# First MLP matrix with three 256-column matmuls per k-tile and a ScalarE rectifier

## The chip, the core and the metric

The kernel runs on one NeuronCore of a Trainium2 chip. The metric is the device time of one execution in microseconds (us), median of several runs; lower is better. Engines are called as in the profile: PE is TensorE (PEld its weight loads), DVE is VectorE, ACT is ScalarE, POOL is GpSimd, SP issues the transfers.

## What is computed

Two layers over 256 tokens of 1024 channels in float32. Each layer has three token mixers (pooling, sparse attention, gated linear attention), a gated merge, an output projection, a squared-ReLU MLP and a gated input embedding. What matters here is the MLP:

```
D_MODEL, SEQ, DEPTH, D_FF = 1024, 256, 2, 4096
h += relu(rmsnorm(h, norm_ffn[i]) @ w_ff1[i]) ** 2 @ w_ff2[i]
```

## The kernel before, in words

Every large product is made of reduced-precision matmuls on split operands: x = high + low, w = high + low, and x·w is taken as high·high + high·low + low·high, all accumulated in PSUM.

Weights come as units of one megabyte (four k-tiles of 128 rows by 512 columns). `prefetch` (L168) loads a unit, `high` (L176) makes the high parts of half a unit on ACT (L180), `low` (L183) the low parts on DVE (L186). At most eight halves are alive (`HL_BUFS`). `step` (L1184) is called after every second k-tile pair of a `Group` and after every `Columns`, and issues at most one low, one high and the loads that are due; so this preparation is interleaved with the rest of each engine's stream, which every engine runs in order.

Two kinds of items run on PE. A `Group` (L1276 to L1278) has the activations as the stationary side and 512 weight columns streaming: three matmuls per k-tile. A `Columns` (L1255 to L1268) is used only for the first MLP matrix. It has 128 weight columns as the stationary side and streams a tile `X[k]` of 512 columns: [high of 256 tokens | low of 256 tokens], made by `norm_x` (L260). Per k-tile it has two matmuls: the weights' high part `wh` against all 512 columns (L1263 or L1266), and the weights' low part `wl` against the first 256 (L1264). So the accumulator `box` takes a whole PSUM bank: columns 0 to 255 hold high·high + low·high, columns 256 to 511 hold high·low.

`hidden(j)` (L1007) makes 512 hidden units: two units of `w_ff1`, four column blocks c, and for each c two `Columns` (kh = 0, 1) of four k-tiles. There are 8 values of j in each of 2 layers, so 16 such blocks of 32 k-tiles. After each c, `post` (L1012) adds the two halves of the bank: ACT copies the second half (L1017), DVE adds the first to it (L1018). After each odd c it works on the pair of column blocks, a tile z of 512: DVE makes max(z, 0)·z (L1020), and `split` makes the high part on ACT (L226) and the low part on DVE (L228). These are `L.f[j, c // 2]`, the stationary side of the second matrix. `ff2_group` (L1026) are Groups for that matrix, into four accumulators `ybox` that stay open for all j. The order of the items is hidden(0), hidden(1), four ff2 groups of j = 0, hidden(2), four ff2 groups of j = 1, and so on, so a block of ff2 groups comes one hidden block after its inputs were begun. Work tiles (`wt`) come from a pool of 47; PSUM has 8 banks.

Of the kernel before, what the change touches and what calls it, by code (L numbers as in the profile page):

```python
# [23 lines left out]

# columns of w_in
C_U, C_Q, C_KV, C_QK, C_V, C_AR, C_GM = 0, 512, 1024, 1816, 2328, 2840, 3368

# columns of the constant tile
K_ID, K_CAUS, K_GLA, K_CMP, K_SEL, K_INV, K_N = 0, 128, 256, 384, 416, 418, 426
# [46 lines left out]
class Unit:  # L76
    """One megabyte of weights, four slots of [128, 512], as high and low parts."""

# [14 lines left out]
class Columns:  # L93
    """128 columns of a unit as the stationary side, the activations of both token tiles streaming"""

# [13 lines left out]
def trunk(tc, x, p, positions, norm_mix, w_in, pool_w, pool_scale, cmp_pos_k, cmp_w_k, cmp_pos_v,  # L109
# [10 lines left out]
    with es:  # L120
# [24 lines left out]

# [1 line left out]
        h = [cp.tile([128, D], F32, name=f"h{t}") for t in range(2)]  # L147
# [13 lines left out]
        def gain(key, k):  # L161
            """a norm's gain, channels [128 k, 128 k + 128)"""
            kind, i = key
            c = 8 * i + k
            return mixg[:, c:c + 1] if kind == "mix" else cols[:, {"ffn": 76, "ple": 92}[kind] + c:][:, 0:1]

# [1 line left out]
        def prefetch(u):  # L168
# [18 lines left out]

# [1 line left out]
        def newton(y, nh, tmp, engine=None, wide=False):  # L189
            """y := (-2 nh)^(-1/2)"""  # L190
            ts(y.bitcast(I32), nh.bitcast(I32), 1, None, op0=ALU.logical_shift_right)
            ts(y.bitcast(I32), y.bitcast(I32), -1, MAGIC, op0=ALU.mult, op1=ALU.add)
            for _ in range(3):
                if engine is not None:
                    engine.tensor_tensor(tmp, y, y, op=ALU.mult)
                    engine.tensor_scalar(tmp, tmp, nh, 1.5, op0=ALU.mult, op1=ALU.add)
                    engine.tensor_tensor(y, y, tmp, op=ALU.mult)
                    continue
                if wide:
                    tt(tmp, y, y, op=ALU.mult)  # L200
                    tt(tmp, tmp, nh, op=ALU.mult)
                else:
                    stt(tmp, y, nh, y, op0=ALU.mult, op1=ALU.mult)
                stt(y, tmp, 1.5, y, op0=ALU.add, op1=ALU.mult)
# [7 lines left out]
        def rstd(s):  # L212
            """s[:, 4:5] := (mean + eps)^(-1/2), the mean being s[:, 1:2] + s[:, 2:3] - eps"""
            ts(s[:, 3:4], s[:, 1:2], s[:, 2:3], -0.5, op0=ALU.add, op1=ALU.mult)
            newton(s[:, 4:5], s[:, 3:4], s[:, 5:6])

        def split_t(src, scale=1.0):
            """transpose of [128 tokens, 512] as four [128, 128], split into high and low"""
            q = ps()
# [12 lines left out]

        # A row's factor 1/rms commutes with the products: rows enter them as h * gain, and what
        # leaves them is scaled on its way out of PSUM.
        aT = {}
# [8 lines left out]
        def gained(q, key, c, out):  # L244
            """high and low parts of q * gain; out(part, k) is where a k-tile's part goes"""
            for part in range(2):
# [13 lines left out]
        def norm_x(t, key, X):  # L260
            """as norm_t, into a tile of [(part, token tile), token] per k-tile, for streaming"""
            for c in range(2):
# [19 lines left out]

# [1 line left out]
        sides = []  # L284
# [36 lines left out]
        def chunk(key, us, post, n=512, ts_=(0, 1), kts=8):  # L321
            """groups of a chunk of n columns over the k-tiles of the units us, one list per token tile"""
            res = []
# [9 lines left out]

# [1 line left out]
        def rope_setup():  # L335
# [41 lines left out]
        def rotate(xv, t):  # L377
            """first 16 of each 64 of [128, 8, 64], in place"""
            tmp = wt().rearrange("p (a n c j) -> p a n c j", a=4, n=8, c=2)
# [5 lines left out]

# [1 line left out]
        def pool_gen(L, i):  # L387
# [32 lines left out]

# [1 line left out]
        def att_gen(L, i):  # L422
# [8 lines left out]
            yield 2  # L431
            # compression blocks: [(parity, d), pair of tokens, key or value, (g, n)], pairs in two tiles
            xs = [wt() for _ in range(2)]
# [3 lines left out]
            for kv in range(2):  # L437
# [14 lines left out]
                yield 1  # L452
            # queries and keys, channels on partitions
            qT = []
# [12 lines left out]
            yield 1  # L467
            # compressed keys (partitions 0-63) and values (64-127), one pass over both weights
            q = ps()
# [27 lines left out]
            def weigh(ev, sm, th):  # L497
                """ev := ev * gate / sum, without the gate's factor 1/2"""
                ts(sm, sm, 1e-30, None, op0=ALU.max)  # L499
# [3 lines left out]

            # compressed branch
            ce = []
            for t in range(2):
# [16 lines left out]
                nc.vector.tensor_reduce(sm, ev, axis=AX.X, op=ALU.add)  # L523
                # the blocks are in (i, g) order, the gates in (g, i) order
                weigh(e.rearrange("p (i g c) -> p i g c", i=4, g=2), sm.rearrange("p (i g) -> p i g", i=4),
# [13 lines left out]

            # selected and window branches  # L540
            work = [(0, g, (2 * a, 2 * a + 1)) for a in range(2) for g in range(2)]
# [74 lines left out]

# [1 line left out]
        def gla_gen(L, i):  # L618
# [62 lines left out]
            for par in range(2):  # L681
# [10 lines left out]
                yield 6  # L692
            # states, one head's rows over its own columns, zeros elsewhere
            state = [wt() for _ in range(3)]
# [64 lines left out]

# [1 line left out]
        def emb_gen(L, i):  # L761
# [9 lines left out]

# [1 line left out]
        def layer(i):  # L773
# [12 lines left out]

            # mixer inputs
            def post_q(t, q):
# [119 lines left out]
            def branch(br, name, attr, first, ns=(0, 1)):  # L908
                for n in ns:
                    if br == 1:  # L910
                        # k-tile i: the heads i and 4 + i
                        wr = w_branch[i, br][:, n * 512:(n + 1) * 512].rearrange("(g i d) n -> g d i n", g=2, i=4)
# [16 lines left out]

            # u, q, ...: inputs of the mixers; G, H, I: gates of the three branches; g, h, i: the branches  # L930
            for c in SEQ:
# [14 lines left out]

            # output projection
            L.mT = {}
# [32 lines left out]

            # product of the input embedding
            X = []
# [19 lines left out]

            # MLP, its hidden units on partitions; 1/rms squared is applied to what it returns
            ybox = {(t, n): Box() for t in range(2) for n in range(2)}

            def hidden(j):  # L1007
                us = two(w_ff1[i], j * 512)
                for c in range(4):
                    box = Box()  # L1010

                    def post(c=c, box=box):  # L1012
                        q = box.ps
                        if c % 2 == 0:
                            L.z = wt()
                        z, zc = L.z, L.z[:, c % 2 * 256:c % 2 * 256 + 256]
                        act(zc, q[:, 256:512], AF.Copy)  # L1017
                        tt(zc, zc, q[:, 0:256], op=ALU.add)  # L1018
                        if c % 2:
                            stt(z, z, 0.0, z, op0=ALU.max, op1=ALU.mult)  # L1020
                            L.f[j, c // 2] = split(z)
                    for kh in range(2):
                        items.append(Columns(us[kh], c, (lambda s, kh=kh: X[4 * kh + s]), (box, 512), kh == 0, kh == 1,
                                             post if kh else None))
# [28 lines left out]

            # gated input embedding
            def post_g(n):
# [8 lines left out]
            def post_last(t, c0, n, box):  # L1064
                """residual, and the final norm of the columns [c0, c0 + n)"""
                s = wt()[:, 0:n]
# [107 lines left out]
        def next_high(n):  # L1174
            """the next half's high part, if it lies near enough and buffers are free"""
            nonlocal n_hi, live
# [17 lines left out]

# [1 line left out]
        mixr = wt()  # L1196
# [49 lines left out]
        for it in items:  # L1246
# [4 lines left out]
            box, n = it.acc  # L1251
            if it.first:
                box.ps_full = ps()
                box.ps = box.ps_full[:, 0:n]
            if isinstance(it, Columns):  # L1255
                cc = slice(it.c * 128, (it.c + 1) * 128)
                for s in range(4):
# [3 lines left out]
                    x = it.rhs(s)  # L1261
                    if s == 0:
                        mm(box.ps, wh, x, start=it.first, stop=False)  # L1263
                    mm(box.ps[:, 0:256], wl, x[:, 0:256], start=False, stop=False)  # L1264
                    if s > 0:
                        mm(box.ps, wh, x, start=False, stop=(it.last and s == 3))  # L1266
                step(at)
# [41 lines left out]
```

## Time and profile before

| | us |
|---|---|
| median of 3 runs | 944.71 |
| lowest and highest | 943.97, 945.86 |
| span of the profiled execution, first to last instruction | 943.0 |
| PE busy, share of the span | 925.8 (98%) |
| DVE busy | 670.5 (71%) |
| ACT busy | 487.7 (52%) |
| both MLP stages, from the first matmul of the first matrix to the last of the second | 174.51 each |

The time of the profiled execution is its span and what lies ahead of the first and behind the last instruction, which the profile does not show. A matmul's row in the trace lasts longer than the time until the next one starts, since they are pipelined: what a matmul costs is read as the distance from its start to the next start. Granted clock 1.00 is 2.4 GHz.

### The profile page before, as it was taken

What the parts mean: (1) busy time and instruction counts of PE and PEld (TensorE: products, weight loads), DVE (VectorE), ACT (ScalarE), POOL (GpSimd) and SP (SyncE); (2) the same over time, 40 slices, a digit from 0 to 9 for tenths busy, and PEclk for the clock granted to TensorE, in tenths of its full rate; (3) what the DMA queues carried; (4) which work ended last, traced back from release to release, by engine and by line L of the source; (5) the groups of instructions that cost most, each with busy time, mean ns of one, the idle gap of its engine ahead of it and who ended that gap; (6) DMA issues with size and microseconds to landing.
All of it is one profiled execution on the core that took longest, in us unless ns stands there. A gap on an engine that the chain in (4) does not pass through costs nothing.

```text
span 943.0 us, 12676 instructions
## 1 busy us (share of the span) xinstructions
PE 925.8 (98%) x4848; PEld 764.5 (81%) x4848; DVE 670.5 (71%) x1203; ACT 487.7 (52%) x833; POOL 16.3 (2%) x37
## 2 busy tenths in 40 slices
PE   6999999999999999999999999999999999999996
PEld 5888877778788888888889887777878888888885
DVE  4976877769667766666886877766885776666675
ACT  5664655454366544444765545544443754555453
POOL 1000000000000000000000000000000000000003
PEclk9999999999999999999999999999999999999998
DMA  7686452336543755555257834534354375555541
GB/s 257 220 257 193 134 167 102 94 94 215 179 163 109 273 201 189 184 199 201 90 151 261 236 95 173 165 119 118 115 198 134 134 243 203 179 179 179 180 154 46
DMA packets 92180, 159.92 MB, mean 170 GB/s; under 512 B 11708, under 2 KB 20056, under 8 KB 92120
## 3 DMA queue, kind: packets, MB, share of 16 engines
q1 hardware_dynamic: 92120, 159.12, 51.1%
q8 instruction: 38, 0.62, 0.3%
q14 instruction: 22, 0.18, 0.1%
HBM read 158.06 MB, written 1.05 MB: 169 GB/s over the span
## 4 chain that ended last, share of the span: by engine, by line
PE 96%; DVE 1%; ACT 1%; DMA 1%; issue 0%; SPq 0%; DVEq 0%
PE ps L1276 22%; PE ps L1278 22%; PE ps L1277 22%; PE ps L1266 10%; PE ps L1264 6%; PE ps L1263 3%; PE ps L600 1%; PE ps L577 1%; PE ps L554 1%; PE ps L241 1%; PE ps L471 1%; PE ps L555 1%; PE ps L556 1%; DMA raw<-in_w_in 1%; PE ps L688 0%; PE ps L726 0%
## 5 line engine op out<-in xcount | busy, mean ns | idle before, releaser
L186 DVE TENSOR_TENSOR lo<-raw,hi 128x1024 fp32r<-128x1024 f32 (+2 forms) x300 | 345.5, 1179 | 37.9 <-ACT hi L180 35.9
L1276 PE MATMUL ps<-hi,w 128*128 128x512 f32 (+3 forms) x952 | 371.0, 390 | 0.5 <-ACT w L226 0.5
L1278 PE MATMUL ps<-hi,w 128*128 128x512 f32 (+3 forms) x952 | 360.5, 379 | 0.9 <-DVE w L230 0.5
L1277 PE MATMUL ps<-lo,w 128*128 128x512 f32 (+3 forms) x952 | 360.7, 379 | 0.6 <-DVE lo L186 0.6
L180 ACT ACTIVATE hi<-raw 128x1024 fp32r<-128x1024 f32 (+2 forms) x300 | 296.3, 1027 | 91.7 <-PE ps L1278 33.8
L1276 PEld LDWEIGHTS ps<-hi,w 128*128 128x128 f32 x952 | 179.3, 188 | 40.4 <-issue 7.8
L1278 PEld LDWEIGHTS ps<-hi,w 128*128 128x128 f32 x952 | 179.2, 188 | 36.2 <-DVE w L230 1.4
L1277 PEld LDWEIGHTS ps<-lo,w 128*128 128x128 f32 x952 | 179.5, 189 | 31.1 <-DVE lo L186 1.5
L1266 PE MATMUL ps<-w,hi 128*128 128x512 f32 x384 | 142.0, 399 | 0.0
L1264 PE MATMUL ps<-w,lo 128*128 128x256 f32 x512 | 123.0, 281 | 0.0
L1264 PEld LDWEIGHTS ps<-w,lo 128*128 128x128 f32 x512 | 96.8, 189 | 10.9
L1266 PEld LDWEIGHTS ps<-w,hi 128*128 128x128 f32 x384 | 72.2, 188 | 11.9
L1018 DVE TENSOR_TENSOR w<-w,ps 128x256 f32<-128x256 f32 x64 | 26.8, 419 | 60.0 <-ACT w L1017 60.0
L566 ACT ACTIVATE w<-ps,mx 128x128 f32<-128x128 f32 (+1 forms) x64 | 26.2, 418 | 69.3 <-DVE mx L562 67.5
L1017 ACT ACTIVATE w<-ps 128x256 f32<-128x256 f32 x64 | 24.4, 385 | 56.7 <-PE ps L1266 56.4
L226 ACT ACTIVATE w<-w 128x512 fp32r<-128x512 f32 x36 | 22.8, 633 | 59.1 <-DVE w L1020 51.4
L1263 PE MATMUL ps<-w,hi 128*128 128x512 f32 x128 | 49.8, 389 | 0.0
L228 DVE TENSOR_TENSOR w<-w,w 128x512 fp32r<-128x512 f32 x36 | 24.9, 693 | 25.3 <-ACT w L226 25.3
L226 ACT ACTIVATE w<-ps 128x512 fp32r<-128x512 f32 x24 | 14.2, 598 | 41.9 <-PE ps L221 24.7
L250 ACT ACTIVATE w<-ps,cols 128x128 fp32r<-128x128 f32 x64 | 17.5, 397 | 32.9 <-PE ps L241 32.9
L499 DVE TENSOR_SCALAR sums<-sums 128x2 f32<-128x2 f32 (+1 forms) x24 | 4.1, 169 | 31.6 <-ACT w L566 31.6
L1263 PEld LDWEIGHTS ps<-w,hi 128*128 128x128 f32 x128 | 24.3, 190 | 0.5
(226 smaller groups left out, 707.0 us busy)
## 6 DMA issues: line engine op xcount, KB each, us to landing
raw<-in_w_ff SPq DMA_DIRECT2D x64, 1024.0 KB, 5.8
raw<-in_w_in SPq DMA_DIRECT2D x42, 1024.0 KB, 5.1
raw<-in_w_branch SPq DMA_DIRECT2D x8, 1024.0 KB, 5.2
raw<-in_w_out SPq DMA_DIRECT2D x8, 1024.0 KB, 5.0
raw<-in_w_ple_gate SPq DMA_DIRECT2D x8, 1024.0 KB, 6.5
raw<-in_w_in SPq DMA_DIRECT2D x8, 528.0 KB, 3.7
raw<-in_w_branch SPq DMA_DIRECT2D x8, 512.0 KB, 6.8
raw<-in_w_in SPq DMA_DIRECT2D x4, 560.0 KB, 4.4
```

Source lines behind the costliest of these rows:

```text
L180: act(hi, u.raw[:, a:b, :], AF.Copy)
L186: tt(lo, u.raw[:, a:b, :], hi.bitcast(F32), op=ALU.subtract)
L226: act(hi, q, AF.Copy, scale=scale)
L228: tt(lo, q, hi.bitcast(F32), op=ALU.subtract)
L566: act(e[:, a * nk:(a + 1) * nk], q[:, a * nk:(a + 1) * nk], AF.Exp, bias=mx[:, a:a + 1], accum_out=sums[t][:, c + a:c + a + 1])
L1018: tt(zc, zc, q[:, 0:256], op=ALU.add)
L1263: mm(box.ps, wh, x, start=it.first, stop=False)
L1264: mm(box.ps[:, 0:256], wl, x[:, 0:256], start=False, stop=False)
L1266: mm(box.ps, wh, x, start=False, stop=(it.last and s == 3))
L1276: mm(box.ps, ah, wh, start=(it.first and j == 0), stop=False)
L1277: mm(box.ps, ah, wl, start=False, stop=False)
L1278: mm(box.ps, al, wh, start=False, stop=(it.last and j == last))
```

## The change

In a `Columns`, each k-tile now has three matmuls of 256 columns that all accumulate into the same 256 columns of PSUM: `wh` against the high half of X, `wh` against its low half, `wl` against the high half. Two column blocks, an even c and the odd one after it, share one PSUM bank (columns 0 to 255 and 256 to 511), and nothing has to be added afterwards. After each odd c, ACT rectifies the whole bank into r, squares r into z, and squares r once more into the high part; DVE subtracts the high part from z for the low part. The copy (L1017), the addition (L1018) and max(z, 0)·z (L1020) go. The file also loses comments, with no effect on the code.

```
             def hidden(j):
                 us = two(w_ff1[i], j * 512)
                 for c in range(4):
-                    box = Box()
-
-                    def post(c=c, box=box):
-                        q = box.ps
-                        if c % 2 == 0:
-                            L.z = wt()
-                        z, zc = L.z, L.z[:, c % 2 * 256:c % 2 * 256 + 256]
-                        act(zc, q[:, 256:512], AF.Copy)
-                        tt(zc, zc, q[:, 0:256], op=ALU.add)
+                    if c % 2 == 0:
+                        both = Box()
+
+                    def post(c=c, both=both):
                         if c % 2:
-                            stt(z, z, 0.0, z, op0=ALU.max, op1=ALU.mult)
-                            L.f[j, c // 2] = split(z)
+                            r, z = wt(), wt()
+                            act(r, both.ps, AF.Relu)
+                            act(z, r, AF.Square)
+                            hi, lo = wt(F32R), wt(F32R)
+                            act(hi, r, AF.Square)
+                            tt(lo, z, hi.bitcast(F32), op=ALU.subtract)
+                            L.f[j, c // 2] = hi, lo
                     for kh in range(2):
-                        items.append(Columns(us[kh], c, (lambda s, kh=kh: X[4 * kh + s]), (box, 512), kh == 0, kh == 1,
+                        items.append(Columns(us[kh], c, (lambda s, kh=kh: X[4 * kh + s]), (both, 512), kh == 0, kh == 1,
                                              post if kh else None))
...
-            if it.first:
+            if it.first and not (isinstance(it, Columns) and it.c % 2):
                 box.ps_full = ps()
                 box.ps = box.ps_full[:, 0:n]
...
                     x = it.rhs(s)
-                    if s == 0:
-                        mm(box.ps, wh, x, start=it.first, stop=False)
-                    mm(box.ps[:, 0:256], wl, x[:, 0:256], start=False, stop=False)
-                    if s > 0:
-                        mm(box.ps, wh, x, start=False, stop=(it.last and s == 3))
+                    o = box.ps[:, it.c % 2 * 256:it.c % 2 * 256 + 256]
+                    mm(o, wh, x[:, 0:256], start=(it.first and s == 0), stop=False)
+                    mm(o, wh, x[:, 256:512], start=False, stop=False)
+                    mm(o, wl, x[:, 0:256], start=False, stop=(it.last and s == 3))
```

## Rows read from the trace of the kernel before

**Rows 1.** The page: busy us, share of the span and instructions of three engines, and the line of engines of the chain of work that ended last.

```profile
PE 925.8 (98%) x4848; PEld 764.5 (81%) x4848; DVE 670.5 (71%) x1203; ACT 487.7 (52%) x833; POOL 16.3 (2%) x37
...
PE 96%; DVE 1%; ACT 1%; DMA 1%; issue 0%; SPq 0%; DVEq 0%
```

**Rows 2.** The waits of the whole execution, those of PE's matmuls: who waited for whom, us in total, times, longest. These are all six.

```profile
PE ps L1231 <- DMA con<-in_cst: 4.4, 1, 4.4
...
PE ps L241 <- DMA h<-in_x: 2.3, 1, 2.3
...
PE ps L1277 <- DVE lo L186: 0.6, 2, 0.4
...
PE ps L1278 <- DVE w L230: 0.5, 2, 0.3
PE ps L1276 <- ACT w L226: 0.5, 2, 0.3
...
PE ps L1278 <- DVE w L252: 0.4, 1, 0.4
```

**Rows 3.** Busy time of each engine in the two MLP stages: stretch, its length, then busy us (instructions) of PE, PEld, DVE, ACT and POOL, the granted clock, the DMA share and GB/s.

```profile
272.19:446.70 174.51, 174.51 (x887) 148.53 (x886) 116.21 (x155) 88.83 (x124) 0.00 (x0) 1.00 0.57 197
733.37:907.88 174.51, 174.51 (x887) 148.51 (x886) 116.21 (x155) 88.70 (x124) 0.00 (x0) 1.00 0.56 196
```

**Rows 4.** The timeline of PE over the first four k-tiles of one hidden block (start, us, line, shape), the start of the next four, and the start of the ff2 groups behind it; then the first matmul of the last hidden block of the second layer and the first behind that.

```profile
305.58 0.39 PE L1263 MATMUL ps<-w,hi 128*128 128x512 f32 x1
...
305.81 0.40 PE L1264 MATMUL ps<-w,lo 128*128 128x256 f32 x2
...
306.04 0.40 PE L1266 MATMUL ps<-w,hi 128*128 128x512 f32 x1
...
306.27 0.28 PE L1264 MATMUL ps<-w,lo 128*128 128x256 f32 x1
...
306.39 0.40 PE L1266 MATMUL ps<-w,hi 128*128 128x512 f32 x1
...
306.63 0.28 PE L1264 MATMUL ps<-w,lo 128*128 128x256 f32 x1
...
306.75 0.40 PE L1266 MATMUL ps<-w,hi 128*128 128x512 f32 x1
...
306.99 0.39 PE L1263 MATMUL ps<-w,hi 128*128 128x512 f32 x1
...
316.83 0.39 PE L1276 MATMUL ps<-hi,w 128*128 128x512 f32 x1
...
877.42 0.39 PE L1263 MATMUL ps<-w,hi 128*128 128x512 f32 x1
...
888.68 0.39 PE L1276 MATMUL ps<-hi,w 128*128 128x512 f32 x1
```

**Rows 5.** The timeline of PE at the end of the second layer, where Groups of 256 weight columns run one behind the other: the first three matmuls of that stretch and the last, 47 starts after the first.

```profile
928.54 0.28 PE L1276 MATMUL ps<-hi,w 128*128 128x256 f32 x1
928.66 0.28 PE L1277 MATMUL ps<-lo,w 128*128 128x256 f32 x1
928.78 0.28 PE L1278 MATMUL ps<-hi,w 128*128 128x256 f32 x1
...
934.18 0.28 PE L1278 MATMUL ps<-hi,w 128*128 128x256 f32 x1
```

**Rows 6.** The timeline of PE over a stretch of 280 columns: its first matmul, and the first behind its 48 matmuls.

```profile
58.23 0.29 PE L1276 MATMUL ps<-hi,w 128*128 128x280 f32 x1
...
64.44 0.40 PE L1276 MATMUL ps<-hi,w 128*128 128x512 f32 x1
```

**Rows 7.** The timeline of PE over matmuls of 32 columns, each with a weight load of 128 columns: the second and the last of twelve.

```profile
86.28 0.26 PE L511 MATMUL ps<-kbs,w 128*128 128x32 f32 x1
...
87.39 0.26 PE L512 MATMUL ps<-kbs,w 128*128 128x32 f32 x1
```

**Rows 8.** Groups of instructions by line and shape, on ACT and DVE: out<-in, count, then busy us and mean ns of one, then idle us just before them and what ended it.

```profile
L1018 DVE TENSOR_TENSOR w<-w,ps 128x256 f32<-128x256 f32 x64 | 26.8, 419 | 60.0 <-ACT w L1017 60.0
L228 DVE TENSOR_TENSOR w<-w,w 128x512 fp32r<-128x512 f32 x36 | 24.9, 693 | 25.3 <-ACT w L226 25.3
L1017 ACT ACTIVATE w<-ps 128x256 f32<-128x256 f32 x64 | 24.4, 385 | 56.7 <-PE ps L1266 56.4
L226 ACT ACTIVATE w<-w 128x512 fp32r<-128x512 f32 x36 | 22.8, 633 | 59.1 <-DVE w L1020 51.4 <-DVE w L417 7.7
L1020 DVE SCALAR_TENSOR_TENSOR w<-w 128x512 f32<-128x512 f32 x32 | 22.1, 692 | 1.1
L226 ACT ACTIVATE w<-ps 128x512 fp32r<-128x512 f32 x24 | 14.2, 598 | 41.9 <-PE ps L221 24.7 <-PE ps L600 8.5 <-PE ps L458 5.6
```

**Rows 9.** The timelines of ACT and of DVE ahead of the third hidden block of the first layer (it begins at 305.58): start, us, line, shape, count, and in brackets the idle time before and what ended it.

```profile
297.53 0.63 ACT L226 ACTIVATE w<-w 128x512 fp32r<-128x512 f32 x1 [5.83 <-DVE w L1020]
...
301.41 5.00 ACT L180 ACTIVATE hi<-raw 128x1024 fp32r<-128x1024 f32 x5
...
302.14 6.89 DVE L186 TENSOR_TENSOR lo<-raw,hi 128x1024 fp32r<-128x1024 f32 x6
```

**Rows 10.** Groups of instructions on ACT: the function-table loads of one line, and the squares: count, busy us, mean ns.

```profile
L857 ACT ACT_TABLE_LOAD x2 | 2.6, 1283 | 0.0
...
L208 ACT ACTIVATE w<-h 128x512 f32<-128x512 f32 x24 | 15.0, 635 | 0.0
```

## The prediction

> **What bounds the kernel now.** I read the page first: PE is busy for 98% of the span and makes up 96% of the chain that ended last, DVE and ACT are at 71% and 52% [rows 1]. Next the waits of PE: six kinds, 8.7 us together, and 6.7 of that is two waits for the first transfers at the start [rows 2]. Then the two stretches that the change touches: in each MLP stage of 174.51 us PE is busy for all of 174.51 us at granted clock 1.00, which is 2.4 GHz, while DVE is busy for 116 and ACT for 89 [rows 3]. So in these stages nothing that ACT or DVE does ends last anywhere. The time there is the sum of the distances from one matmul start to the next, and a change of it must come from PE's stream, or from a wait of PE that is not there now.
>
> **The matmuls, before.** The timeline gives the price [rows 4]. Four k-tiles of a hidden block run from 305.58 to 306.99, 1.41 us for eight matmuls. A whole block of 32 k-tiles runs from 305.58 to 316.83, 11.25 us, and the last one of the second layer from 877.42 to 888.68, 11.26. With 11.255 as the mean, the 16 blocks take 180.1 us.
>
> **The matmuls, after.** A k-tile streams the same 768 columns, in three instructions in place of two: 512 k-tiles, so 1536 matmuls of 256 columns in place of 512 of 512 and 512 of 256. The question is what each 256-column matmul costs in a row of such. The kernel already has that pattern, at its end: the Groups of 256 columns have, per k-tile, the same stationary tile twice and then another, every time 256 columns streaming into the same 256 columns of PSUM, just as the new Columns. There 928.54 to 934.18 holds 47 steps: 5.64/47 = 0.1200 us each, and the step behind the repeated stationary tile (928.54 to 928.66) is no shorter than the others [rows 5]. That this is a price per matmul beside its columns is seen at other widths. 48 matmuls of 280 columns take 6.21 us, 0.1294 each [rows 6]; at 2.4 GHz 280 columns alone are 0.1167 and 256 are 0.1067, so each leaves about 13 ns that do not shrink with the width. The new stream therefore takes 1536 x 0.1200 = 184.3 us, against 180.1: **4.2 us more**, which is the 512 added matmuls with their fixed share, less some 20 ns per four k-tiles by which the mixed order of wide and narrow was dearer than its parts.
>
> **Bounds of that price.** From below: twelve matmuls of only 32 columns with the same 128-column weight load follow each other at (87.39 - 86.28)/10 = 0.111 us [rows 7], so with a load for each, which the trace shows for every matmul (as many PEld as PE, [rows 1]), none will be under 0.111: 1536 x 0.111 = 170.5, a gain of 9.6. Nearer is the pair of narrow matmuls in today's Columns, 305.81 to 306.04 for two, 0.115 to 0.117 with the rounding of the rows [rows 4]: 1536 x 0.1165 = 178.9, a gain of 1.2. From above, the 280-column price gives 1536 x 0.1294 = 198.8, a loss of 18.7, but this has 24 columns too many. I take 0.1200, since rows 5 have the width, the order and the accumulation of the new stream, and 47 steps of it; the pair has one narrow neighbour and lies between wide ones. The decision lies at 180.1/1536 = 0.1173 us: below it the stream gains.
>
> The Trainium skill ("TensorE: Matmul & The Clock Gate", Back-to-back issue gap) states N/2.4 plus about 2.5 ns as the distance of warm matmuls. By that alone 512 more matmuls would cost 512 x 2.5 ns = 1.3 us, a time of 946.0; rows 5 and 6 disagree, with about 13 ns.
>
> **ACT and DVE.** Per pair of column blocks (32 pairs) the old code has on ACT two copies of 385 ns and the high part of 633 ns, 1.40 us; on DVE two additions of 419, the max-product of 692 and the low part of 693, 2.22 us [rows 8]. The new code has a rectification of 512 columns out of PSUM, for which I take the 598 ns of L226 out of PSUM, and two squares at the 633 to 635 ns of an SBUF pass [rows 8, 10]: 1.87 us on ACT, and 0.69 on DVE. So ACT gains 0.46 us per pair, 7.4 us per stage, and goes from 89 to 96 of some 177 us; DVE loses 1.53 per pair, 24.5 us per stage. Neither is on the path: both changes count as nothing, covered by PE's stream. If that cover were gone, ACT's would cost at most 32 x 0.46 = 15 us.
>
> Rectification runs nowhere in this trace, so its table could matter. Squares already run, with no load of their own; the loads that there are, as the one ahead of L857 in each layer, take 1.283 us [rows 10]. Between zero and two loads per pair would be 0 to 32 x 2.57 = 82 us of ACT time, 41 per stage, and 137 of 177 would still fit. I take none. The Trainium skill ("ScalarE: Activation LUTs", Table sets: the hidden batching unit) says that cheap functions, relu among them, are in every set.
>
> **The waits that go and come.** Today ACT waits for the sum and the product on DVE before each high part, 51.4 us in all [rows 8]; that wait goes, since r, z and the high part are all ACT's and follow PE's last matmul of the pair. What is queued behind them on ACT is the weights' high parts, and behind DVE's wait for the high part the weights' low parts. This queue is what PE would feel. Its tightest place: ACT stood 5.83 us for DVE up to 297.53, made five high parts from 301.41, and DVE six low parts from 302.14 in 6.89 us [rows 9]. The first four are for the block that begins at 305.58; the fourth ends at about 302.14 + 4 x 1.15 = 306.7, and PE comes to it at 306.99 + 0.69 = 307.7, the third k-tile of the second four. That is a lead of 1 us. The new order takes ACT's 5.83 us away and adds 0.46, so the lead grows. The new low part waits on DVE for three ACT passes in a row, 1.87 us, with low parts of weights behind it; but DVE has 1.53 us less of its own per pair and no longer waits for the copies (60.0 us in all, [rows 8]). What is late next is therefore nothing on PE's side: f is wanted a block of 11 us later.
>
> **PSUM and work tiles.** Two banks per block in place of four, each read by one ACT pass; four work tiles per pair in place of three, two of them free again within the pair, out of 47. Nothing, since a wait for either would be ACT's, under the cover above. Transfers, hooks and the number of `step` calls are unchanged.
>
> **The sum.** Against the profiled execution: 943.0 + 4.2 = 947.2 us of span. The median 944.71 lies 1.7 above that span, which I keep: 948.9 us, +0.45%. About 0.2% (1.9 us) is what a measurement here can tell from no change.
>
> **Rivals.**
> 1. The narrow matmuls cost what today's pair costs, 0.1165 us, so that the extra instructions are paid by the end of the mixed order. Place: every hidden block; point: 0.1173 us per matmul. It gives 944.7 - 1.2 = 943.5, no slower than before. For it: the pair's own rows; against: 47 steps of rows 5. Chance 0.07. The skill's rule above ends in the same class, at 946.0.
> 2. The change does not add what it says: the second matmul on the same stationary tile needs no load of its own and hides its fixed 13 ns. 512 such: 184.3 - 6.8 = 177.5, a gain of 2.6, 942.1. Rows 5 have the same repetition, with no shorter step. Chance 0.03.
> 3. ACT's longer work makes weight parts late: PE begins to wait for hi or lo at the heads of hidden blocks. With the whole of ACT's addition on the path, 948.9 + 15 = 964; with 1 us at four blocks, 953. For it: the lead of 1 us; against: ACT's 51.4 us of waits that go. Chance 0.05.
>
> **How the numbers follow.** The forecast has 0.85. Its own width: 0.1200 is known to some 0.0004 (0.6 us), the runs of before spread by -0.7 and +1.2 us, and I allow a microsecond for each of the edges between narrow and wide stretches and a small new wait: 946 to 951, which leaves out rivals 1 to 3 and a little of the forecast, 0.18 in all. Slower by over 0.2% (above 946.6): most of the forecast and rival 3, 0.88. Within 0.2%: rival 1 and the forecast's low end, 0.09. Faster: rival 2, 0.03.
>
> **What would show it.** In the profile after, the first matmuls of a hidden block should start 0.12 us apart, a hidden block should take 11.52 us in place of 11.25, an ff2 block the same as before, and each MLP stage 176.6. PE should have no waits there; DVE should fall by some 49 us, ACT rise by some 15, with no more table loads. It is wrong if the step is under 0.1185, or if PE has gaps ahead of L1276 or the new lines.

## The result, and the profile after

The changed kernel takes 949.94 us, median of 4 runs (949.5 to 950.77), against 944.89 for the kernel before: a ratio of 1.0053, interval 1.0042 to 1.0065. It is slower by half a per cent, 5.05 us; 948.9 us was forecast. Four executions that took between 1862 and 3249 us, three of the kernel before and one of the last experiment, are left out of all times and ratios.

The page has PE as the bound as before; DVE has 47 us less work than in [rows 1], ACT 13 us more.

```profile
PE 930.1 (98%) x5360; PEld 791.7 (84%) x5360; DVE 623.3 (66%) x1107; ACT 500.9 (53%) x833; POOL 16.3 (2%) x37
...
PE 97%; DVE 1%; ACT 1%; DMA 1%; SPq 0%; issue 0%; DVEq 0%
```

PE's instructions went from 4848 to 5360, the 512 added matmuls. Its waits are those of [rows 2], none of them in the MLP (who waited for whom, us in total, times, longest; these are all six):

```profile
PE ps L1231 <- DMA con<-in_cst: 4.3, 1, 4.3
PE ps L241 <- DMA h<-in_x: 2.4, 1, 2.4
PE ps L1275 <- ACT w L226: 0.5, 2, 0.3
PE ps L1277 <- DVE w L230: 0.5, 2, 0.2
PE ps L1277 <- DVE w L252: 0.4, 1, 0.4
PE ps L1276 <- DVE lo L186: 0.4, 1, 0.4
```

In the two MLP stages (stretch, length, then busy us of PE, PEld, DVE, ACT, POOL, granted clock, DMA share, GB/s) PE is busy from end to end, as in [rows 3]:

```profile
271.87:448.49 176.62, 176.62 (x1141) 161.93 (x1140) 92.45 (x107) 95.55 (x124) 0.00 (x0) 1.00 0.56 195
735.32:911.95 176.63, 176.63 (x1142) 161.95 (x1141) 92.44 (x107) 95.44 (x124) 0.00 (x0) 1.00 0.56 194
```

Measured from the first matmul of the first matrix to the first transposition behind the last of the second, as here, the stages took 174.35 us before (the rows of [rows 3] end 0.16 later). So each stage has become 2.27 us longer, 4.54 together. PE's timeline says where. It is shown for the same hidden block as in [rows 4]: its first four matmuls, then the first and the sixth of the ff2 block behind it, and the start of the next hidden block. The last two rows are the two ends of the last hidden block of the second layer:

```profile
305.81 0.28 PE L1263 MATMUL ps<-w,hi 128*128 128x256 f32 x1
305.92 0.28 PE L1264 MATMUL ps<-w,hi 128*128 128x256 f32 x1
306.04 0.28 PE L1265 MATMUL ps<-w,lo 128*128 128x256 f32 x1
306.16 0.28 PE L1263 MATMUL ps<-w,hi 128*128 128x256 f32 x1
...
317.32 0.40 PE L1275 MATMUL ps<-hi,w 128*128 128x512 f32 x1
...
318.48 0.39 PE L1277 MATMUL ps<-hi,w 128*128 128x512 f32 x1
...
328.23 0.28 PE L1263 MATMUL ps<-w,hi 128*128 128x256 f32 x1
...
881.36 0.28 PE L1263 MATMUL ps<-w,hi 128*128 128x256 f32 x1
...
892.87 0.40 PE L1275 MATMUL ps<-hi,w 128*128 128x512 f32 x1
```

Both blocks take 11.51 us, 0.120 per matmul, where they took 11.25 and 11.26. Eight blocks per stage are 2.08 of the 2.27 us. The rest is at the seams: an ff2 block behind a hidden block takes 10.91 us (317.32 to 328.23) against 10.88, seven times per stage. That, too, is seen in PE's starts: the first five matmuls of 512 columns take 1.16 us (317.32 to 318.48), where five at the ff2 blocks' mean of 0.2267 take 1.13; in ns, by the starts in the trace, they are 233, 236, 228, 233 and 231 apart, and from the sixth on 226 or 227. In the kernel before, a wide matmul stands ahead of the ff2 block, and its steps are 226 or 227 from the first on.

The new operations (groups by line and shape: count, busy us, mean ns, then the idle time before them and what ended it):

```profile
L1016 ACT ACTIVATE w<-ps 128x512 f32<-128x512 f32 x32 | 19.1, 596 | 74.9 <-PE ps L1265 74.9
L1017 ACT ACTIVATE w<-w 128x512 f32<-128x512 f32 x32 | 20.2, 632 | 1.0
L1019 ACT ACTIVATE w<-w 128x512 fp32r<-128x512 f32 x32 | 19.6, 613 | 0.0
L1020 DVE TENSOR_TENSOR w<-w,w 128x512 fp32r<-128x512 f32 x32 | 22.2, 692 | 133.0 <-ACT w L1019 133.0
```

The three passes take ACT 1.84 us per pair, where 1.87 was forecast. ACT now waits for PE alone ahead of L1016, and not for DVE; DVE's wait for L1019, 133 us in all, is where its freed time went, and PE has no wait there.

### The profile page after: what moved, and what is told of

The parts are those of the page before. It is cut to its first block, busy times and chain, and to the rows that moved or that the text cites. A ratio compares the mean times of both kernels' runs of the same rounds, so it can differ in the third digit from the quotient of the medians.

```text
span 947.2 us, 13648 instructions
## 1 busy us (share of the span) xinstructions
PE 930.1 (98%) x5360; PEld 791.7 (84%) x5360; DVE 623.3 (66%) x1107; ACT 500.9 (53%) x833; POOL 16.3 (2%) x37
## 4 chain that ended last, share of the span: by engine, by line
PE 97%; DVE 1%; ACT 1%; DMA 1%; SPq 0%; issue 0%; DVEq 0%
PE ps L1275 22%; PE ps L1277 21%; PE ps L1276 21%; PE ps L1265 6%; PE ps L1264 6%; PE ps L1263 6%; PE ps L600 1%; PE ps L577 1%; PE ps L241 1%; PE ps L554 1%; PE ps L471 1%; PE ps L555 1%; PE ps L556 1%; DMA h<-in_x 1%; PE ps L688 0%; PE ps L726 0%
## 5 line engine op out<-in xcount | busy, mean ns | idle before, releaser
L1265 PE MATMUL ps<-w,lo 128*128 128x256 f32 x512 | 145.1, 283 | 0.0
L1264 PE MATMUL ps<-w,hi 128*128 128x256 f32 x512 | 145.0, 283 | 0.0
L1263 PE MATMUL ps<-w,hi 128*128 128x256 f32 x512 | 145.0, 283 | 0.0
L1020 DVE TENSOR_TENSOR w<-w,w 128x512 fp32r<-128x512 f32 x32 | 22.2, 692 | 133.0 <-ACT w L1019 133.0
L1263 PEld LDWEIGHTS ps<-w,hi 128*128 128x128 f32 x512 | 98.3, 192 | 0.5
L1264 PEld LDWEIGHTS ps<-w,hi 128*128 128x128 f32 x512 | 98.3, 192 | 0.5
L1016 ACT ACTIVATE w<-ps 128x512 f32<-128x512 f32 x32 | 19.1, 596 | 74.9 <-PE ps L1265 74.9
L252 DVE SCALAR_TENSOR_TENSOR w<-ps,cols,w 128x128 fp32r<-128x128 f32 x64 | 17.3, 344 | 8.4 <-ACT w L250 8.4
L857 ACT ACTIVATE w<-ps,st 128x512 f32<-128x512 f32 x24 | 16.4, 684 | 9.8 <-PE ps L1277 6.4
```

What stands on the lines that cost most here:

```text
L1016: act(r, both.ps, AF.Relu)
L1020: tt(lo, z, hi.bitcast(F32), op=ALU.subtract)
L1263: mm(o, wh, x[:, 0:256], start=(it.first and s == 0), stop=False)
L1264: mm(o, wh, x[:, 256:512], start=False, stop=False)
L1265: mm(o, wl, x[:, 0:256], start=False, stop=(it.last and s == 3))
```

## The experiments

Each was timed beside the kernel before on the same chip; ratios stand with their 95% interval. In the code, `...` stands for lines left out.

**The changed kernel again.** No edit.

> The changed kernel once more, beside the others. Theory: the whole cost is 512 added matmuls, 4.2 us of PE's stream, and nothing else. Then this is 4 to 5 us above the kernel before, 949 to 950, with hidden blocks of 11.51 us against 11.25. Rival: part of the 5.05 us that were measured (4.2 explained, 0.8 not) comes from the ScalarE part.

It took 949.49 us against 945.05, ratio 1.0044 (1.0030 to 1.0058): 4.4 us by the medians. The first measurement had 5.05, and the two agree within their intervals. Of the 0.8 us of the first that the hidden blocks do not explain, 0.4 is at the seams (14 times 0.027), and 0.3 lies outside the span: the time there was 2.3 us in the runs of the changed kernel and 2.0 in those of the kernel before. What is left is within the spread of medians of four or five runs.

**The matmuls alone.** The new matmuls, with rectification and square on DVE and the high part copied by ACT.

```
-                            r, z = wt(), wt()
-                            act(r, both.ps, AF.Relu)
-                            act(z, r, AF.Square)
-                            hi, lo = wt(F32R), wt(F32R)
-                            act(hi, r, AF.Square)
-                            tt(lo, z, hi.bitcast(F32), op=ALU.subtract)
-                            L.f[j, c // 2] = hi, lo
+                            z = wt()
+                            ts(z, both.ps, 0.0, None, op0=ALU.max)
+                            tt(z, z, z, op=ALU.mult)
+                            L.f[j, c // 2] = split(z)
```

> The new matmuls with the old sharing of work: DVE rectifies (0.6 to 0.7 us out of PSUM) and squares, ACT copies the high part, DVE subtracts. Theory (only the matmul count matters): the same as the changed kernel, within 0.5 us of it, hidden blocks 11.51 us. Rival (the ScalarE part carries 0.8 us): 0.8 us below the changed kernel.

It took 949.38 us, ratio 1.0043 (1.0030 to 1.0056), with DVE back at 666 us and ACT down to 465. A hidden block, from its first matmul to the first behind it, is as long as in the changed kernel, to the rounding of the rows (11.51 or 11.52 us):

```profile
305.49 0.28 PE L1260 MATMUL ps<-w,hi 128*128 128x256 f32 x1
...
317.01 0.40 PE L1272 MATMUL ps<-hi,w 128*128 128x512 f32 x1
```

So the cost is in the matmuls, to within the noise.

**The ScalarE part alone.** The old matmuls, the old copy and addition, then three ACT passes.

```
-                            stt(z, z, 0.0, z, op0=ALU.max, op1=ALU.mult)
-                            L.f[j, c // 2] = split(z)
+                            r = wt()
+                            act(r, z, AF.Relu)
+                            z = wt()
+                            act(z, r, AF.Square)
+                            hi, lo = wt(F32R), wt(F32R)
+                            act(hi, r, AF.Square)
+                            tt(lo, z, hi.bitcast(F32), op=ALU.subtract)
+                            L.f[j, c // 2] = hi, lo
```

> The old matmuls and the old copy and addition, but rectification, square and high part on ACT as in the change: ACT gets 32 x 1.25 = 40 us more than before, more than the change itself gives it. Theory (ACT is hidden under PE): the same as the kernel before within 0.5 us, hidden blocks 11.25 us. Rival (ScalarE part costs): 0.8 us or more above before; if ACT's work made weights late, PE would show waits for hi or lo.

It took 946.20 us against 945.05, ratio 1.0011 (1.0002 to 1.0020): a miss for the theory. All hidden blocks but one per layer take 11.25 to 11.26 us; the third takes 11.86 (305.38 to 317.24). PE's timeline has a gap in it, the only one there, in brackets with its releaser:

```profile
307.24 0.39 PE L1272 MATMUL ps<-w,hi 128*128 128x512 f32 x1
308.00 0.39 PE L1270 MATMUL ps<-w,lo 128*128 128x256 f32 x1 [0.36 <-DVE lo L186]
```

The timelines of ACT and DVE ahead of it, to be read beside [rows 9]:

```profile
297.06 0.63 ACT L1021 ACTIVATE w<-w 128x512 f32<-128x512 f32 x1 [5.10 <-DVE w L1018]
```

```profile
302.71 0.69 DVE L1026 TENSOR_TENSOR w<-w,w 128x512 fp32r<-128x512 f32 x1 [1.89 <-ACT w L1025]
303.32 6.89 DVE L186 TENSOR_TENSOR lo<-raw,hi 128x1024 fp32r<-128x1024 f32 x6
```

This is the place that was named as the tightest. ACT waits for DVE's sum (L1018, which this kernel keeps), then makes three passes in place of one, for which DVE waits 1.89 us at a time. So the low parts begin at 303.32 where they began at 302.14, 1.18 us later than before, for a block that begins 0.2 us earlier. That is more than the lead of 1 us; the fourth of them is late for the third k-tile of the second four. In the changed kernel the same place is far from late (its ACT timeline, then its DVE timeline):

```profile
292.82 1.06 ACT L180 ACTIVATE hi<-raw 128x1024 fp32r<-128x1024 f32 x1 [0.50 <-PE ps L1264]
...
296.79 1.05 ACT L180 ACTIVATE hi<-raw 128x1024 fp32r<-128x1024 f32 x1
...
299.76 2.01 ACT L180 ACTIVATE hi<-raw 128x1024 fp32r<-128x1024 f32 x2 [1.92 <-DMA raw<-in_w_ff]
```

```profile
297.53 2.35 DVE L186 TENSOR_TENSOR lo<-raw,hi 128x1024 fp32r<-128x1024 f32 x2
300.85 2.36 DVE L186 TENSOR_TENSOR lo<-raw,hi 128x1024 fp32r<-128x1024 f32 x2 [0.97 <-ACT hi L180]
```

Its four low parts are done by 303.2, 2.6 us ahead of the block at 305.81. PE uses the fourth in that block's 21st matmul, 20 steps of 0.120 us later, at 308.2: a lead of 5.0 us, where the prediction found 1 us in the kernel before (306.7 and 307.7).

**The same with later norms.** The last kernel, with `norm_s` moved from behind the first hidden block to j = 3.

```
...
-            hook(norm_s, 0, kffn)
-            hook(norm_s, 1, kffn)
             for j in range(nj):
+                if j == 3:
+                    hook(norm_s, 0, kffn)
+                    hook(norm_s, 1, kffn)
```

> The kernel with the old matmuls and the ACT part alone, and the two norms of the MLP's input taken three blocks later (they are wanted only at the end of the MLP). Theory (that kernel's third hidden block waits 0.6 us per layer because the norms and ACT's waits for DVE's sums pile up ahead of the weights' low parts): the wait goes, hidden blocks all 11.25 to 11.26 us, 1.2 us below that kernel, level with the kernel before. Rival (ACT's added passes alone make the low parts late): the 11.86 us of the third block stay, or come back at the block of the norms.

It took 944.66 us against 945.14, ratio 0.9997 (0.9988 to 1.0005); every hidden block takes 11.25 to 11.26, the third one too (305.01 to 316.27). So the wait needs two things together: the norms, whose 22 small DVE operations stand ahead of the sums that ACT waits for, and ACT's added passes. The kernel before has the norms alone there, this kernel the passes alone, and neither waits. At j = 3, where norms and passes meet in this kernel, PE does not wait either: the six low parts behind the norms begin 7.3 us ahead of the hidden block at 371.41, where in the last kernel they began 2.1 us ahead (303.32 and 305.38).

```profile
364.06 7.15 DVE L186 TENSOR_TENSOR lo<-raw,hi 128x1024 fp32r<-128x1024 f32 x6
```

**Other columns.** The old accumulator of 512 columns, but the wide matmul cut in two in six of eight k-tiles, 384 added matmuls that do not all fall into the same columns.

```
-                    if s == 0:
-                        mm(box.ps, wh, x, start=it.first, stop=False)
+                    first, last = it.first and s == 0, it.last and s == 3
+                    if first:
+                        mm(box.ps, wh, x, start=True, stop=False)
+                    elif not last:
+                        mm(box.ps[:, 0:256], wh, x[:, 0:256], start=False, stop=False)
+                        mm(box.ps[:, 256:512], wh, x[:, 256:512], start=False, stop=False)
                     mm(box.ps[:, 0:256], wl, x[:, 0:256], start=False, stop=False)
-                    if s > 0:
-                        mm(box.ps, wh, x, start=False, stop=(it.last and s == 3))
+                    if last:
+                        mm(box.ps, wh, x, start=False, stop=True)
```

> The old kernel, its accumulator of 512 columns and its post kept, but in six of the eight k-tiles of a column block the wide matmul is cut in two of 256 columns, which go to different columns of PSUM: 384 added matmuls in place of 512. Theory (the price is per matmul): per column block 2 x 0.2267 + 20 x 0.1200 = 2.853 us against 2.814, 64 blocks, 2.5 us above the kernel before. Rival (what the change pays for is that all three matmuls accumulate into the same 256 columns): no slower than before.

It took 948.03 us, ratio 1.0033 (1.0021 to 1.0045), 3.0 us slower where 2.5 was expected; a hidden block takes 11.40 us, 0.14 more than before, where the sum gave 0.16:

```profile
306.91 0.39 PE L1264 MATMUL ps<-w,hi 128*128 128x512 f32 x1
...
318.31 0.40 PE L1280 MATMUL ps<-hi,w 128*128 128x512 f32 x1
```

The cost comes with the count, whichever columns of PSUM are written.

**No repeated stationary tile.** The changed kernel with the order high·high, low·high, high·low in even k-tiles and high·low, low·high, high·high in odd ones.

```
-                    mm(o, wh, x[:, 0:256], start=(it.first and s == 0), stop=False)
-                    mm(o, wh, x[:, 256:512], start=False, stop=False)
-                    mm(o, wl, x[:, 0:256], start=False, stop=(it.last and s == 3))
+                    if s % 2 == 0:
+                        mm(o, wh, x[:, 0:256], start=(it.first and s == 0), stop=False)
+                        mm(o, wl, x[:, 0:256], start=False, stop=False)
+                        mm(o, wh, x[:, 256:512], start=False, stop=False)
+                    else:
+                        mm(o, wh, x[:, 256:512], start=False, stop=False)
+                        mm(o, wl, x[:, 0:256], start=False, stop=False)
+                        mm(o, wh, x[:, 0:256], start=False, stop=(it.last and s == 3))
```

> The changed kernel with the order of the three matmuls turned so that no stationary tile comes twice in a row inside a k-tile. Theory (a matmul costs its columns plus 13 ns, whether its stationary tile is the one before or another): the same as the changed kernel, hidden blocks 11.51 us. Rival (the repeated tile saves its load or part of the 13 ns): up to 6.8 us slower than the changed kernel.

It took 949.37 us, ratio 1.0051 (1.0037 to 1.0066), with hidden blocks of 11.51 us as in the changed kernel:

```profile
305.48 0.28 PE L1264 MATMUL ps<-w,hi 128*128 128x256 f32 x1
...
316.99 0.40 PE L1280 MATMUL ps<-hi,w 128*128 128x512 f32 x1
```

Repeating the stationary tile saves nothing.

**128 columns in one of four k-tiles.** The changed kernel with each of the three matmuls of k-tile s = 1 cut in two.

```
-                    mm(o, wh, x[:, 0:256], start=(it.first and s == 0), stop=False)
-                    mm(o, wh, x[:, 256:512], start=False, stop=False)
-                    mm(o, wl, x[:, 0:256], start=False, stop=(it.last and s == 3))
+                    for w, x0, begin, end in ((wh, 0, it.first and s == 0, False), (wh, 256, False, False),
+                                              (wl, 0, False, it.last and s == 3)):
+                        for m in ((0, 128), (128, 256)) if s == 1 else ((0, 256),):
+                            mm(o[:, m[0]:m[1]], w, x[:, x0 + m[0]:x0 + m[1]], start=begin, stop=end)
```

> The changed kernel, but in one of four k-tiles each of the three matmuls is cut in two of 128 columns: 384 more matmuls, no more columns. Theory A (13 ns per matmul, nothing else): 6 x 0.0667 = 0.400 us per such k-tile against 0.360, 128 of them, 5.1 us above the changed kernel. Theory B (each matmul waits for a weight load of its own, which takes 0.111 us as the 32-column matmuls showed): 0.667 against 0.360, 39 us above the changed kernel.

It took 988.48 us, ratio 1.0463 (1.0449 to 1.0476): 39 us above the changed kernel, theory B to the microsecond. In PE's timeline the six pieces of 128 columns run from 310.68 to 311.29, and the two matmuls of 256 columns behind them to 311.59 (merged by line and operand, count at the end):

```profile
310.68 0.56 PE L1266 MATMUL ps<-w,hi 128*128 128x128 f32 x4
...
311.07 0.39 PE L1266 MATMUL ps<-w,lo 128*128 128x128 f32 x2
311.29 0.46 PE L1266 MATMUL ps<-w,hi 128*128 128x256 f32 x2
311.59 0.28 PE L1266 MATMUL ps<-w,lo 128*128 128x256 f32 x1
```

The timeline of PEld has the weight loads of the same stretch:

```profile
310.56 0.54 PEld L1266 LDWEIGHTS ps<-w,hi 128*128 128x128 f32 x4
311.01 0.30 PEld L1266 LDWEIGHTS ps<-w,lo 128*128 128x128 f32 x2
311.24 0.30 PEld L1266 LDWEIGHTS ps<-w,hi 128*128 128x128 f32 x2
```

A hidden block takes 13.97 us against 11.51, so a k-tile with six pieces costs 0.36 + 2.46/8 = 0.667 us, 0.111 per piece. The rows of the six alone have 0.61 us; the rest falls on the two behind them, which take 0.30 in place of 0.24. The loads begin 0.11 us apart there (four from 310.56 to 311.01), although 128 columns at 2.4 GHz are 0.053. The price is that of the 32-column matmuls in [rows 7], which share the 128-column weight load. So at 128 columns a matmul of such a row costs its weight load, and the 256 columns of the change, at 0.120, are only just above that. That it is the load, and not another fixed price per matmul, is read from these rows; no experiment changed the size of the load.

**Wide matmuls side by side.** The old kernel, per `Columns` first four wide and then four narrow ones, and in the next the other way round.

```
...
+                for lows in ((False, True) if it.first else (True, False)):
+                    for s in range(4):
...
+                        if lows:
+                            mm(box.ps[:, 0:256], lo[:, s % 2, cc], x[:, 0:256], start=False, stop=False)
+                        else:
+                            mm(box.ps, hi[:, s % 2, cc], x, start=(it.first and s == 0), stop=(it.last and s == 3))
```

> The old kernel with the same matmuls in another order: in a Columns first the four wide (512) matmuls and then the four narrow (256) ones, in the next Columns of the same accumulator first the narrow and then the wide. Theory (each matmul costs its columns at 2.4 GHz plus 13 ns, and changing between wide and narrow costs some 20 ns per four k-tiles today): 8 x 0.2267 + 8 x 0.1200 = 2.774 us per column block against 2.814, 64 blocks, 2.6 us faster than before, about 942.3. Rival (narrow matmuls side by side cost the 0.1165 of today's pair): 4.4 us faster. Rival (order is free): no change.

It took 944.00 us against 945.05, ratio 0.9987 (0.9978 to 0.9996): faster than both kernels, by less than half of what was expected. The chain of work that ended last shows the four wide matmuls that open a hidden block, and further on two stretches of wide and one of narrow ones (start, us, line, count):

```profile
327.79 0.91 PE ps L1265 x4
...
332.44 1.84 PE ps L1265 x8
334.28 0.95 PE ps L1263 x8
335.23 1.84 PE ps L1265 x8
```

Narrow ones cost 0.119 us, but wide ones 0.230, not the 0.2267 of Groups. The four that open the block stand behind the wide matmuls of a Group, and they do cost 0.227. The starts in the trace tell the two apart: in the 50 runs of eight wide matmuls behind eight narrow ones, the mean steps are 233, 236, 228, 232 and 231 ns, and 227 from the sixth on; in the four that open a block they are 227 at once. It is the same row of steps as at the seams of the changed kernel. A hidden block is 11.17 us, 0.085 less than before, and 1.15 us less in all 16.

**Wide and narrow in turn.** The old kernel, with the wide matmul first in each k-tile.

```
-                    if s == 0:
-                        mm(box.ps, wh, x, start=it.first, stop=False)
+                    end = it.last and s == 3
+                    if not end:
+                        mm(box.ps, wh, x, start=(it.first and s == 0), stop=False)
                     mm(box.ps[:, 0:256], wl, x[:, 0:256], start=False, stop=False)
-                    if s > 0:
-                        mm(box.ps, wh, x, start=False, stop=(it.last and s == 3))
+                    if end:
+                        mm(box.ps, wh, x, start=False, stop=True)
```

> The old kernel with the same matmuls, strictly wide, narrow, wide, narrow (the last two of a column block the other way round). Theory (a wide matmul behind a narrow one costs more than one behind a wide one): 0.356 us per k-tile as in the rows of before, 2.2 us slower than before. Rival (order is free, and the grouped kernel gained elsewhere): no change.

It took 945.68 us, ratio 1.0005 (0.9996 to 1.0014); hidden blocks are 11.27 us against 11.255. That is 0.3 us in all 16, and not the 2.2 us that were expected: a k-tile takes 11.27/32 = 0.352 us. The 0.356 was rightly read, as the mean of the three pairs of a narrow and a wide matmul in four k-tiles of before (306.27 to 306.63 is one, [rows 4]); but it is a price among those neighbours, and with others ahead of them the same pairs cost less.

**Groups without a repeated stationary tile.** The old kernel with the second and third matmul of every Group exchanged.

```
-                    mm(box.ps, ah, wl, start=False, stop=False)
-                    mm(box.ps, al, wh, start=False, stop=(it.last and j == last))
+                    mm(box.ps, al, wh, start=False, stop=False)
+                    mm(box.ps, ah, wl, start=False, stop=(it.last and j == last))
```

> The old kernel with the three 512-column matmuls of every Group in the order high·high, low·high, high·low, so that no stationary tile comes twice in a row (952 k-tiles of them, none in the first MLP matrix). The grouped kernel showed wide matmuls of the first matrix, each with a new stationary tile, at 0.230 us, and those of Groups, where one in three repeats the tile before, cost 0.2267. Theory (a repeat makes no difference, as in the narrow matmuls): no change. Rival (a new stationary tile costs up to 5 ns more than a repeated one): 952 x 0.005 us = up to 5 us slower, ff2 blocks above 10.88 us.

It took 945.35 us against 945.14, ratio 1.0005 (0.9996 to 1.0014), with ff2 blocks of 10.88 us as before. So a new stationary tile is not what makes the wide matmuls of the first matrix dearer than those of Groups; the grouped kernel's trace shows that the narrow ones ahead of them are.

## Why the prediction was right

**The bound.** It was read as PE's stream alone, since the MLP stages had PE busy for their whole length. After the change it is so again, and the kernel with the new matmuls and the old sharing of work took 949.38 beside the 949.49 of the changed kernel. Shown.

**The price per matmul.** 0.1200 us was taken from the last Groups of the kernel before [rows 5], and 1536 x 0.1200 = 184.3 us. Measured: 16 blocks of 11.51 to 11.515 us, 184.2. The rivals fell with it: the pair's price of 0.1165, and the repeated stationary tile, which was tried in both kinds of items and saves nothing. The pair's price was that of two narrow matmuls just behind a wide one, 113 and 119 ns by the starts in the trace; those further on cost 120. The rule that the prediction cites from the Trainium skill ("TensorE: Matmul & The Clock Gate", Back-to-back issue gap), N/2.4 plus 2.5 ns, which that section gives for an isolated matmul, leads to an estimate of 946.0 us; the runs do not agree, with 949.94 and 949.49. That it is the count, and not the columns that are accumulated, was shown by 384 added matmuls in the old layout.

**"Price beside the columns", 13 ns.** The number holds at the 256, 280 and 512 columns that were read; at widths between it was not tested. At 128 columns it fails: there the weight load rules, at 0.111 us, as the lower bound of the prediction had it.

**The mixed order.** The blocks before were dearer than the sum of their parts by 20 ns per four k-tiles, and the prediction put this down to the mixed order of wide and narrow matmuls. The traces bear it out. In the grouped kernel a wide matmul of the first matrix costs 227 ns behind wide ones, and 228 to 236 as one of the first five behind eight narrow ones, with the same operands; the first two narrow ones behind wide ones cost 113 and 119 in place of 120. What does not hold is a price that goes with the number of changes, which the expectations of the two reordered kernels took for granted. One change to eight narrow matmuls and back to eight wide ones still costs some 23 ns. So the grouped kernel, with a sixth of the changes, keeps 11 of the 20 ns per four k-tiles, and the strictly alternating one has 23. Why a wide matmul is dearer behind narrow ones is open.

**ACT and DVE at nothing.** Right, and by the mechanism that was given: the wait of ACT for DVE's sums went, and the lead of the weights' low parts at the tightest place grew from 1 to 5.0 us. The rival that the low parts come late was a real danger at the very place named: with the ACT passes added and the sums kept it happened, 0.6 us in each layer, and moving the norms took it away. No table load was added (seven before and after).

**The sum.** 948.9 was forecast and 949.94 measured, 949.49 the second time. The blocks gave 4.2 us as forecast. Two terms were not in the sum. The seams (0.027 us at 14 ff2 blocks, 0.4 us) are wide matmuls behind narrow ones; only the range allowed for such edges. The time outside the span was kept at 1.7 us, from a span and a median of different runs, but the runs have 2.0 before and 2.3 after. The 0.3 goes neither with the new matmuls alone (1.9 in that kernel) nor with the ACT part alone (1.9), but every kernel here that has both has 2.3; its cause is open.

## What to carry to other kernels

Where PE is busy from end to end of a stage, a change of that stage is priced by the distance between matmul starts, and the number of matmuls counts beside their columns: two of 256 cost 0.240 us where one of 512 costs 0.227, or 0.228 to 0.236 as one of the first five behind narrower ones. Look for the new pattern elsewhere in the same trace before pricing it by a rule, and take the mean of many steps of that very pattern: prices read off a few steps among other neighbours (0.1165, 0.356) did not carry over. Relief of an engine that has no one waiting for it is worth nothing, but it moves the lead of what is queued behind it, so look for the place where that lead is smallest.

## What the runs showed that was not expected

- A matmul of 128 or 32 columns with a 128-column weight load costs the same 0.111 us; at 256 it is 0.119 to 0.120. Cutting one k-tile in four down to 128 columns cost 39 us.
- A matmul of 512 columns costs 0.2267 us in a row of such, but 233, 236, 228, 232 and 231 ns as one of the first five behind eight or more 256-column ones, at the same granted clock of 1.00. It happens in the first MLP matrix and in the Groups of the ff2 blocks alike.
- The order of wide and narrow matmuls is worth a little: runs of eight wide and eight narrow gave 944.00 us, the fastest time of this study.
